# A two-layer RWKV-7 and attention trunk on one core: group norm over eight heads at once, one output-weight pass less, transposes held back

## The chip, the cores and the metric

The kernel runs on one core of one Trainium2 chip. Five engines work side by side: TensorE (PE in the profile; its weight loads are PEld), VectorE (DVE), ScalarE (ACT), GpSimd (POOL) and SyncE (SP), which issues most of the DMAs. The metric is the device time of one execution in microseconds (us); of the kernel before, three runs are known, with a median of 740.5 us.

## The reference

The input is 256 tokens of 1024 numbers. Layer 0 is an RWKV-7 time mix and a SwiGLU feed-forward, layer 1 is attention and a second feed-forward; behind each of the four stands a layer norm over `ALPHA * x + sublayer(x)`. The part that matters here is the end of the time mix and the start of the first feed-forward:

```python
_, y = lax.scan(step, S0, ...)                       # recurrence over 256 tokens, 16 heads of 64
mean = y.mean(-1, keepdims=True)                     # group norm: per token and head
var = jnp.square(y - mean).mean(-1, keepdims=True)
y = ((y - mean) * lax.rsqrt(var + GN_EPS)).reshape(B, T, C) * gn_g + gn_b
bonus = jnp.sum(rh * kh * r_k, -1, keepdims=True) * vh
y = (y + bonus.reshape(B, T, C)).astype(x.dtype)
h = (y * g) @ w_o
...
x = layer_norm(ALPHA * x + h, ln_mix_g[i], ln_mix_b[i])
gate, up = jnp.split(x @ w_in, 2, axis=-1)
x = layer_norm(ALPHA * x + (silu(gate) * up) @ w_down, ln_ffn_g[i], ln_ffn_b[i])
```

## The kernel before

**Split weights.** Every product is made in three parts to keep float32 accuracy: a weight block of 512 KB lands in a buffer `raw` (three of them in a ring), ACT casts it to a high part `hi`, and DVE or POOL makes the low part `lo = raw - hi`. The activations have the same two parts (`xhi`, `xlo`; or `xw` with both). TensorE then adds hi by xhi, lo by xhi and hi by xlo. `Stream` does this for a list of blocks in a fixed order (`weight_specs`). A block of kind "split" uses one of four rotating pairs of hi and lo buffers, so the fifth such block waits until the first has been used for the last time; a block of kind "keep" has buffers of its own. `PL` says which blocks POOL makes the low part of, `LATER` which low parts wait for a named event, and `W.hold` which blocks are not cast before a named event.

**Time mix.** The recurrence goes over four chunks of 64 tokens and two groups `f` of eight heads; TensorE makes z, u, s and y of each step, ACT and DVE copy them out (`UV`, `S`, `zs`, `y`). Tokens are handled in two halves `hf` of 128. `group_norm(hf, f)` normalises y of one half and one group of eight heads: with `bn_stats` and `bn_aggr` head by head, a root on ACT, a subtraction and a product on DVE; then TensorE transposes the result (`yt`), DVE multiplies by the gate `gT` and adds `Q` (`yg`), and the two parts are written to `xs0` (`xhi`, `xlo`).

**Output product and norm.** `dense0` multiplies `xs0` by the output weights `w_o` (`wo0`): for each half eight blocks (two column halves `cb` by four row quarters `q`), 48 matmuls of 512 columns into two banks `o`. In the kernel before, the four blocks of `cb` 1 are kept for both halves, and the four of `cb` 0 are loaded and split twice. `norm_and_turn` then does the layer norm on DVE in `xtok` (a token half at a time), and each normalised 512 columns are transposed by TensorE (`tr`) and split into `xw`.

**First feed-forward.** The first four blocks of `in0` are the weights of the first two hidden tiles; they are multiplied token half by token half (`gn`, 48 matmuls of 256 columns for each half), and from there on come matmuls of both halves at once (`gu`, `acc`). `hidden_half` makes the activation of the first two tiles and transposes it (`ht`).

**Order of the work.** A planner (`Issue.run`) sets the order in which instructions are issued. Work is written as generators that yield what they wait for; at each step the planner takes, of those that are ready by its own clock (`Clock`), the one of the lowest rank (the first number of `I.add`). `fence` makes the later instructions of an engine stand behind the earlier ones in the built program. Each engine runs its instructions in this fixed order, so one that waits holds all behind it.

Of the kernel before, what the change touches and what calls it, by code (L numbers as in the profile page):

```python
# [65 lines left out]
BON = 'pool'  # L66
BONW = 'T'
ORDERED = False
PL = {'wo1': [], 'in1': [], 'qkv': [7, 11], 'wo0': [1, 2, 4, 6], 'k': [2], 'r': [0], 'v': [2, 3, 4, 5, 6, 7], 'g2': [0, 1], 'w2': [], 'in0': [5]}
LATER = {'wo0': {11: 'n00'}, 'in0': {0: 'x10'}, 'qkv': {3: 'n10', 4: 'x21', 5: 'x21', 6: 'x21'}, 'in1': {0: 'n20', 1: 'x30', 2: 'x30', 3: 'x30'}}  # L70
LD = {}
MIXV = 'pool'
MIXG = 'pool'
# [326 lines left out]
def weight_specs(a):  # L400
    assert FIRST <= LAG <= min(TAIL)
    specs = []

    def s1(name, key, idx, kind="split", cols=128):
        specs.append((name, kind, KT, cols, 128, a[key][idx]))

    def s2(name, key, cb, kind="split"):
        for q in range(4):
            specs.append((name, kind, 2, 512, 128, a[key][cb * 4 + q]))

    def ffn(i):
        for n in range(2 * FIRST):
            specs.append((f"in{i}", "split", 4, 256, 128, a[f"w_if{i}"][n]))
        for j in range(FIRST, NJ):
            for u in range(2):
                s1(f"in{i}", f"w_in{i}", (j - FIRST) * 2 + u)
            if LAG <= j < NJ - TAIL[i] + LAG:
                specs.append((f"down{i}", "split", 1, 1024, 128, a[f"w_dn{i}"][j - LAG]))
        for j in range(NJ - TAIL[i], NJ):
            specs.append((f"down{i}", "keep", 1, 1024, 128, a[f"w_dn{i}"][j]))  # L420

    for p in range(KT):
        s1("k", "w_k", p, "native" if p < 2 else "split")
        if p == W2AT:
            for n in range(2):
                specs.append(("w2", "keep", 1, 1024, 128, a["w_2"][n]))
        if p == SELAT:
            specs.append(("sel", "cast", KT, 128, 48, a["selT"]))
    for p in range(KT):
        s1("r", "w_r", p)  # L430
    s2("v", "w_v", 0)
    s1("g1", "w_g1a", 0, "native")
    s1("g1", "w_g1b", 0, "native", 96)
    specs.append(("g2", "split", 1, 1024, 128, a["w_g2a"]))
    specs.append(("g2", "stack", 1, 1024, 96, a["w_g2b"]))
    s2("v", "w_v", 1)
    s2("wo0", "w_o0", 0)
    s2("wo0", "w_o0", 1, "keep")
    s2("wo0", "w_o0", 0)
    ffn(0)  # L440
    for n, cb in enumerate((0, 2, 4, 1, 3, 5)):
        s2("qkv", "w_qkv", cb, "keep" if n == 0 else "split")
    for q in range(4):
        for cb in range(2):
            specs.append(("wo1", "keep" if HELD <= q and not (RING and q >= 2) else "split", 2, 512, 128, a["w_o1"][cb * 4 + q]))
    ffn(1)
    return specs
# [3 lines left out]
def trunk(ctx, tc, a, out):  # L451
# [16 lines left out]
    def nm(s):  # L468
        uid[0] += 1
        return f"{s}{uid[0]}"  # L470
# [16 lines left out]
    def ev(name):  # L487
        return E.setdefault(name, Event())
# [4 lines left out]
    for i in range(2):  # L493
        at = [n for n, x in enumerate(W.specs) if x[0] == f"in{i}"][0]
        nxt = [n for n in range(at + 2 * FIRST, len(W.specs)) if W.specs[n][1] == "split"]
        for n in range(2 * FIRST):
            W.hold[nxt[n]] = ev(f"held{i}{n}")

# [148 lines left out]
                I.reach(end, x)  # L647
            yield 0.0

    def norm_and_turn(ev_in, hps, x, gb, xs, half, done, cuts, end=None):  # L650
        yield ev_in
        if len(xs) == 4:
            parts = [(x[:, :, 0, TOK[half]], x[:, :, 1, TOK[half]]) for x in xs]
        else:
            parts = [(x[0][:, :, TOK[half]], x[1][:, :, TOK[half]]) for x in xs]
        m = len(parts) // 2
        fin = count(2 * m, lambda: I.reach(done, *(x[1] for x in parts)))

        def turned(q):
            def part():  # L660
                yield x[:, q * 512:(q + 1) * 512]
                v = turn(x, q, "tr")
                for n in range(m):
                    I.add(1, split(*parts[q * m + n], v[:, n * 4 // m:(n + 1) * 4 // m, :], done=fin))
            I.add(1, part())
        yield from layer_norm(hps, x, gb, cuts, turned, end)
# [538 lines left out]
    xs0 = pieces()  # L1205

    def group_norm(hf, f):
        st = sm.tile([128, 8, 6], F32, tag="gst", name=nm("gst"))
        mv = sm.tile([128, 8, 2], F32, tag="gmv", name=nm("gmv"))
        rs = sm.tile([128, 8], F32, tag="grs", name=nm("grs"))  # L1210
        y = yt[hf][:, f * 8:f * 8 + 8, :]
        yield ev(f"y{hf}{f}")
        for h0 in range(0, 8, 4):
            yield I.idle("DVE")
            for h in range(h0, h0 + 4):
                dve.bn_stats(st[:, h, :], y[:, h, :])
            for h in range(h0, h0 + 4):
                dve.bn_aggr(mv[:, h, :], st[:, h, :])
        yield mv
        act.activation(rs, mv[:, :, 1], AF.Sqrt, bias=eps_gn, scale=1.0)  # L1220
        dve.tensor_tensor(y, y, mv[:, :, 0:1].to_broadcast([128, 8, HD]), ALU.subtract)
        yield rs
        dve.reciprocal(rs, rs)
        dve.tensor_tensor(y, y, rs[:, :, None].to_broadcast([128, 8, HD]), ALU.mult)
        yield y
        yield ev(f"Q{hf}{f}")
        v = turn(yt[hf].rearrange("p h d -> p (h d)"), f, "yt")
        yield v
        m = sm.tile([128, 4, 128], F32, tag="w2", name=nm("yg"), bufs=6)
        dve.tensor_tensor(m, v, gT[f][:, :, TOK[hf]], ALU.mult)  # L1230
        dve.tensor_tensor(m, m, Q[f][:, :, TOK[hf]], ALU.add)
        xh, xl = (x[:, :, TOK[hf]] for x in xs0[f])
        yield from split(xh, xl, m)
        I.reach(ev(f"xy{hf}{f}"), xl)
# [56 lines left out]
    def dense0():  # L1291
# [99 lines left out]
        for hf in range(2):  # L1391
            res[hf] = [bank("o") for _ in range(2)]
            todo = [(0, q) for q in range(4)] + [(1, q) for q in range(4)]
            if hf == 1:
                todo = [(cb, q) for q0 in (0, 2) for cb in (1, 0) for q in (q0, q0 + 1)]
            for cb, q in todo:
                yield ev(f"xy{hf}{q // 2}")
                if (hf, cb) == (1, 1):
                    w = kept[q]
                else:  # L1400
                    w = yield from W.get("wo0")
                    if cb == 1:
                        kept.append(w)
                mm_s2(res[hf][cb], w, xs0, q * 2, hf, q == 0, q == 3)
                yield 0.0
            if xn is None:
                yield ev("rec")
                l0.close()
                pools["fp"] = ctx.enter_context(tc.tile_pool(name="fp", bufs=2))
                xn = wide_pieces()  # L1410
            I.add(1, norm_and_turn(ev(f"h0{hf}"), res[hf][::1 - 2 * hf], xtok[hf], gb, xn, hf, ev(f"x1{hf}"), WIDE[::1 - 2 * hf], ev(f"n0{hf}")))
            I.reach(ev(f"h0{hf}"), *res[hf])
        return xn, xtok

# [1 line left out]
    def ffn(i, xs, evs, finish):  # L1416
# [62 lines left out]
        for hf in range(2):  # L1479
            ps = bank("gn")[:, :FIRST * 256]  # L1480
            for n in range(2 * FIRST):
                if hf == 0:
                    ws.append((yield from W.get(f"in{i}")))
                if n == 0:
                    yield evs[hf]
                j, q = n // 2, n % 2
                m = 0
                for k in range(4):
                    x = xs[q * 2 + k // 2][:, k % 2]
                    for ww, xx in ((ws[n][0], x[:, 0]), (ws[n][1], x[:, 0]), (ws[n][0], x[:, 1])):  # L1490
                        mm(ps[:, j * 256:(j + 1) * 256], xx[:, TOK[hf]], ww[:, k, :],
                           start=(q + m == 0), stop=(q == 1 and m == 11))
                        m += 1
                if hf == 1:
                    I.reach(ev(f"held{i}{n}"))
                yield 0.0
            I.add(1, hidden_half(hf, ps))
        for j in range(FIRST, NJ):
# [102 lines left out]
    def dense1(xs, xtok):  # L1601
# [59 lines left out]
                    yield 0.0  # L1661
        xn = wide_pieces()
        for hf in range(2):
            I.add(1, norm_and_turn(ev(f"h1{hf}"), res[hf], xtok[hf], gb, xn, hf, ev(f"x3{hf}"), WIDE, ev(f"n2{hf}")))
            if hf == 1:
                for cb in range(2):
                    for q in range(HELD, 4):
                        out_part(hf, q, cb)
                        yield 0.0
            I.reach(ev(f"h1{hf}"), *res[hf])  # L1670
# [52 lines left out]
    I.add(6, bonus())  # L1723
    for hf in range(2):
        for f in range(2):
            I.add(7, group_norm(hf, f))
    I.add(30, dense())
    I.run()

# [82 lines left out]
```

## Time and profile before

| | us |
|---|---|
| runs | 739.4, 740.5, 740.72 |
| profiled execution, its own time | 739.19 |
| its span, first to last instruction | 737.4 |
| PE busy | 681.3 (92%) |
| DVE busy | 531.4 (72%) |
| ACT busy | 392.9 (53%) |
| POOL busy | 139.3 (19%) |

The times in the profile run from the span's first instruction, so the span is what moves when the chain of waits gets shorter, and 1.8 us lie around it. A share of busy time is a mean over stages with different limits; the chain that ended last is 67% PE and 19% DVE. The mean clock granted to TensorE is 0.969 of full speed.

### The profile page before, as it was taken

The numbers are of one execution on the slowest core, as the hardware profiler recorded it, in microseconds if no ns is written. First come the engines' busy times: TensorE is split into PE (matmuls) and PEld (weight loads), VectorE is DVE, ScalarE is ACT, GpSimd is POOL, SyncE is SP. The second block draws the span as 40 slices with busy tenths as digits, with TensorE's granted clock in tenths as the row PEclk, the third lists the DMA queues.
The fourth block names the chain that finished last, engine by engine and source line by source line (L and its number), as shares of the span: only waits on it lengthen the run. The fifth ranks groups of instructions, "written<-read, shape, count | busy, mean of one in ns | idle before, by whom it ended". The sixth has DMA issues, their size and how long they took to land.

```text
span 737.4 us, 11797 instructions
## 1 busy us (share of the span) xinstructions
PE 681.3 (92%) x4500; PEld 582.2 (79%) x4500; DVE 531.4 (72%) x933; ACT 392.9 (53%) x712; POOL 139.3 (19%) x111
## 2 busy tenths in 40 slices
PE   6899695898787999999999899999989999999995
PEld 5899684777667888888888677777778888888885
DVE  7989999839995756656567945968587666656566
ACT  5984454565353554554556435766646555454550
POOL 5677964451400100000000023110000000000000
PEclk9999898899997999999999999999999999999998
DMA  6445313030564655555556545346046565555541
GB/s 245 154 146 191 105 33 115 30 116 33 174 207 152 228 187 184 197 182 192 196 178 229 172 147 178 133 140 200 2 172 213 189 198 179 191 183 189 199 145 57
DMA packets 33576, 117.21 MB, mean 159 GB/s; under 512 B 3808, under 2 KB 4832, under 8 KB 33520
## 3 DMA queue, kind: packets, MB, share of 16 engines
q1 hardware_dynamic: 31936, 110.89, 45.4%
q10 hardware_dynamic: 1584, 5.57, 2.2%
q8 instruction: 35, 0.57, 0.3%
q14 instruction: 21, 0.17, 0.1%
HBM read 115.40 MB, written 1.05 MB: 158 GB/s over the span
## 4 chain that ended last, share of the span: by engine, by line
PE 67%; DVE 19%; DMA 5%; ACT 3%; issue 3%; POOL 2%; DVEq 0%; SPq 0%; ACTq 0%; POOLq 0%
PE gu L328 29%; PE acc L328 14%; PE qkv L328 8%; DVE lo L328 4%; PE gn L328 3%; PE o L328 3%; DVE TT L328 2%; DVE tmp L328 2%; ACT hi L328 2%; PE k L328 2%; DVE xtok L328 1%; DMA raw<-in_w_qkv_dram 1%; DMA raw<-in_w_dn_dram 1%; DVE mx L328 1%; PE pv L328 1%
## 5 line engine op out<-in xcount | busy, mean ns | idle before, releaser
L328 DVE TENSOR_TENSOR lo<-raw,hi 128x1024 fp32r<-128x1024 f32 (+1 forms) x193 | 231.8, 1208 | 151.4 <-ACT hi L328 151.0
L328 ACT CAST hi<-raw 128x1024 fp32r<-128x1024 f32 (+1 forms) x213 | 211.9, 1002 | 174.2 <-issue 78.5
L328 PE MATMUL gu<-xw,hi 128*128 128x512 f32 x640 | 226.0, 394 | 0.0
L328 PE MATMUL gu<-xw,lo 128*128 128x256 f32 x640 | 180.4, 282 | 0.0
L328 PEld LDWEIGHTS gu<-xw,hi 128*128 128x128 f32 x640 | 120.2, 188 | 26.6
L328 PEld LDWEIGHTS gu<-xw,lo 128*128 128x128 f32 x640 | 120.5, 188 | 0.8
L328 POOL TENSOR_TENSOR lo<-raw,hi 128x1024 fp32r<-128x1024 f32 (+1 forms) x20 | 41.6, 2088 | 240.0 <-ACT hi L328 239.5
L328 PE MATMUL acc<-hi,hh 128*128 128x512 f32 (+1 forms) x180 | 53.7, 368 | 0.3 <-ACT hh L328 0.3
L328 PE MATMUL acc<-lo,hh 128*128 128x512 f32 (+1 forms) x180 | 53.7, 368 | 0.0
L328 PE MATMUL acc<-hi,hl 128*128 128x512 f32 (+1 forms) x180 | 53.7, 368 | 0.0
L328 PE MATMUL qkv<-hi,xhi 128*128 128x512 f32 x96 | 39.9, 416 | 2.7 <-ACT xhi L328 2.7
L328 ACT ACTIVATE silu<-silu 128x256 f32<-128x256 f32 x40 | 16.7, 418 | 44.0 <-DVE silu L328 44.0
L328 PE MATMUL qkv<-lo,xhi 128*128 128x512 f32 x96 | 38.6, 402 | 0.0
L328 PE MATMUL qkv<-hi,xlo 128*128 128x512 f32 x96 | 38.6, 402 | 0.0
L328 PEld LDWEIGHTS acc<-hi,hl 128*128 128x128 f32 x180 | 32.8, 188 | 6.3 <-DVE hl L328 0.2
L328 PEld LDWEIGHTS acc<-lo,hh 128*128 128x128 f32 x180 | 32.7, 188 | 5.9
L328 PEld LDWEIGHTS acc<-hi,hh 128*128 128x128 f32 x180 | 31.7, 188 | 6.5 <-ACT hh L328 0.7
L328 PE MATMUL o<-hi,xhi 128*128 128x512 f32 x64 | 26.1, 416 | 2.8 <-ACT xhi L328 2.8
L328 PE MATMUL gn<-hi,xw 128*128 128x256 f32 x128 | 27.0, 307 | 0.1
L328 PE MATMUL o<-hi,xlo 128*128 128x512 f32 x64 | 25.8, 403 | 1.2 <-DVE xlo L328 1.2
L328 PE MATMUL o<-lo,xhi 128*128 128x512 f32 x64 | 26.5, 413 | 0.0
L328 PEld LDWEIGHTS qkv<-hi,xhi 128*128 128x128 f32 x96 | 18.5, 193 | 6.9 <-ACT xhi L328 2.9
(229 smaller groups left out, 1258.1 us busy)
## 6 DMA issues: line engine op xcount, KB each, us to landing
raw<-in_w_in_dram SPq DMA_DIRECT2D x80, 512.0 KB, 3.4
raw<-in_w_dn_dram SPq DMA_DIRECT2D x44, 512.0 KB, 3.4
raw<-in_w_qkv_dram SPq DMA_DIRECT2D x24, 512.0 KB, 3.5
raw<-in_w_o_dram SPq DMA_DIRECT2D x20, 512.0 KB, 3.4
raw<-in_w_r_dram SPq DMA_DIRECT2D x8, 512.0 KB, 3.3
raw<-in_w_v_dram SPq DMA_DIRECT2D x8, 512.0 KB, 3.3
raw<-in_w_if_dram SPq DMA_DIRECT2D x8, 512.0 KB, 3.4
raw<-in_w_k_dram SPq DMA_DIRECT2D x6, 512.0 KB, 3.4
```

The lines of the kernel that those rows point to most:

```text
L328: ins = f(*args, **kw).ins
```

## The change

Three things are changed, and they are all between the recurrence and the second token half of the first feed-forward tiles (one line does the same for layer 1).

1. `group_norm` sums over eight heads at once: one `tensor_reduce` over 128x512 gives the sums, one `scalar_tensor_tensor` subtracts the means, ACT squares the result, a second `tensor_reduce` sums the squares. For the first token half its rank goes from 7 to 4, ahead of the recurrence with 5.
2. The `wo0` blocks are eight and not twelve: all are used for both token halves. Of these POOL splits two, and not four. The first four `in0` blocks are held until the second half's products of `cb` 0 have been issued.
3. The transposes of the second token half wait (`gate`) until the `gn` products of the first half have been issued, with fences on PE; those of the first half wait for a place in the last output products.

```diff
-PL = {..., 'wo0': [1, 2, 4, 6], ...}
-LATER = {'wo0': {11: 'n00'}, 'in0': {0: 'x10'}, ...}
+PL = {..., 'wo0': [1, 2], ...}
+LATER = {'in0': {0: 'x10', 1: 'x10'}, ...}
...
     s2("wo0", "w_o0", 0)
     s2("wo0", "w_o0", 1, "keep")
-    s2("wo0", "w_o0", 0)
...
+        for n in range(4 if i == 0 else 0):
+            W.hold[at + n] = ev(f"held2{n}")
...
-    def norm_and_turn(ev_in, hps, x, gb, xs, half, done, cuts, end=None):
+    def norm_and_turn(ev_in, hps, x, gb, xs, half, done, cuts, end=None, gate=None):
...
+                if gate is not None:
+                    yield gate
                 yield x[:, q * 512:(q + 1) * 512]
...
-        for h0 in range(0, 8, 4):
-            yield I.idle("DVE")
-            for h in range(h0, h0 + 4):
-                dve.bn_stats(st[:, h, :], y[:, h, :])
-            for h in range(h0, h0 + 4):
-                dve.bn_aggr(mv[:, h, :], st[:, h, :])
-        yield mv
-        act.activation(rs, mv[:, :, 1], AF.Sqrt, bias=eps_gn, scale=1.0)
-        dve.tensor_tensor(y, y, mv[:, :, 0:1].to_broadcast([128, 8, HD]), ALU.subtract)
+        yield I.idle("DVE")
+        dve.tensor_reduce(st, y, AX.X, ALU.add)
+        dve.scalar_tensor_tensor(y, st[:, :, None].to_broadcast([128, 8, HD]), -1.0 / HD, y, ALU.mult, ALU.add)
+        yield y
+        sq = sm.tile([128, 8, HD], F32, tag="w2", name=nm("gsq"), bufs=6)
+        act.activation(sq, y, AF.Square)
+        yield sq
+        dve.tensor_reduce(rs, sq, AX.X, ALU.add)
+        yield rs
+        act.activation(rs, rs, AF.Sqrt, bias=eps_gn, scale=1.0 / HD)
...
-                todo = [(cb, q) for q0 in (0, 2) for cb in (1, 0) for q in (q0, q0 + 1)]
+                todo = [(cb, q) for q0 in (0, 2) for cb in (0, 1) for q in (q0, q0 + 1)]
...
-                if (hf, cb) == (1, 1):
-                    w = kept[q]
+                if hf == 1:
+                    w = kept[cb * 4 + q]
                 else:
                     w = yield from W.get("wo0")
-                    if cb == 1:
-                        kept.append(w)
+                    kept.append(w)
                 mm_s2(res[hf][cb], w, xs0, q * 2, hf, q == 0, q == 3)
+                if (hf, cb) == (1, 0):
+                    I.reach(ev(f"held2{q}"))
+                if (hf, cb, q) == (1, 1, 2):
+                    pe.fence()
+                    I.reach(ev("o00"))
+                if hf == 1 and (cb, q) == todo[-1]:
+                    pe.fence()
...
-            I.add(1, norm_and_turn(..., res[hf][::1 - 2 * hf], ..., WIDE[::1 - 2 * hf], ev(f"n0{hf}")))
+            I.add(1, norm_and_turn(..., res[hf], ..., WIDE, ev(f"n0{hf}"), ev("gn0") if hf else ev("o00")))
...
                 if hf == 1:
                     I.reach(ev(f"held{i}{n}"))
+                elif n == 2 * FIRST - 1:
+                    pe.fence()
+                    I.reach(ev(f"gn{i}"))
...
-            I.add(1, norm_and_turn(ev(f"h1{hf}"), ..., WIDE, ev(f"n2{hf}")))
+            I.add(1, norm_and_turn(ev(f"h1{hf}"), ..., WIDE, ev(f"n2{hf}"), ev("gn1") if hf else None))
...
-            I.add(7, group_norm(hf, f))
+            I.add(7 if hf else 4, group_norm(hf, f))
```

In the built program the rows of every engine are the same in both kernels up to the recurrence's third chunk, and again from the second half's `gn` products on. In between, three places move. The first is DVE at the end of the recurrence. `UV_140<-u` is the copy by which the recurrence's last chunk goes on; the second of the two (u_2100 before, u_2103 now) is DVE's last instruction of the recurrence; y_141 and y_142 are the token halves, and xlo_148 is the first operand of the output product that DVE writes. Before:

```order
L328 SCALAR_TENSOR_TENSOR Q_145<-bo_2069,vec,gT_143 128x128 x2
L328 COPY UV_140<-u_2100 64x256
L328 SCALAR_TENSOR_TENSOR Q_145<-bo_2069,vec,gT_143 128x128 x2
L328 TENSOR_TENSOR y_141<-y_141,grs_175 128x512
L328 BN_STATS gst_176<-y_142 128x6 x4
L328 BN_AGGR gmv_177<-gst_176 128x2 x4
L328 BN_STATS gst_176<-y_142 128x6 x2
L328 SCALAR_TENSOR_TENSOR Q_146<-bo_2152,vec,gT_144 128x128 x4
L328 TENSOR_TENSOR yg_2198<-yt_2188,gT_143 128x512
L328 TENSOR_TENSOR yg_2201<-yt_2193,gT_144 128x512
L328 TENSOR_TENSOR yg_2198<-yg_2198,Q_145 128x512
L328 TENSOR_TENSOR yg_2201<-yg_2201,Q_146 128x512
```

Now:

```order
L328 TENSOR_TENSOR yg_2059<-yt_2039,gT_143 128x512
L328 TENSOR_TENSOR y_141<-y_141,grs_172 128x512
L328 TENSOR_TENSOR yg_2059<-yg_2059,Q_145 128x512
L328 COPY UV_140<-u_2050 64x256
L328 TENSOR_TENSOR yg_2112<-yt_2097,gT_144 128x512
L328 TENSOR_TENSOR xlo_148<-yg_2059,xhi_147 128x4x128
L328 TENSOR_TENSOR yg_2112<-yg_2112,Q_146 128x512
L328 COPY UV_140<-u_2103 64x256
L328 SCALAR_TENSOR_TENSOR Q_145<-bo_1949,vec,gT_143 128x128 x4
L328 TENSOR_REDUCE gst_174<-y_142 128x8
```

The first half's `yg` and xlo_148 have moved from behind the recurrence's last copy to ahead of it, and the 128x6 and 128x2 instructions are gone.

The second place is TensorE at the layer norm (xtok_2216 before and xtok_2140 now are the second token half; gn_2502 and gn_2422 are the first half's feed-forward products, gn_2495 the second half's). Before:

```order
L328 MATMUL o_2379<-hi_2412,xlo_150 128x512
L328 MATMUL o_2379<-hi_2412,xhi_149 128x512
L328 MATMUL o_2379<-lo_2413,xhi_149 128x512
L328 MATMUL o_2379<-hi_2412,xlo_150 128x512
L328 MATMUL tr_2528<-cst,xtok_2216 128x128 x4
L328 MATMUL tr_2536<-cst,xtok_2216 128x128 x4
L328 MATMUL gn_2502<-hi_2423,xw_2375 128x256
L328 MATMUL gn_2502<-lo_2424,xw_2375 128x256
L328 MATMUL gn_2502<-hi_2423,xw_2375 128x256 x2
L328 MATMUL gn_2502<-lo_2424,xw_2375 128x256
```

Now:

```order
L328 MATMUL gn_2422<-lo_2424,xw_2304 128x256
L328 MATMUL gn_2422<-hi_2423,xw_2304 128x256 x2
L328 MATMUL gn_2422<-lo_2424,xw_2304 128x256
L328 MATMUL gn_2422<-hi_2423,xw_2304 128x256
L328 MATMUL tr_2498<-cst,xtok_2140 128x128 x4
L328 MATMUL tr_2508<-cst,xtok_2140 128x128 x4
L328 MATMUL ht_2513<-cst,sg_2496 128x128 x2
L328 MATMUL gn_2495<-hi_2277,xw_2301 128x256
L328 MATMUL gn_2495<-lo_2278,xw_2301 128x256
L328 MATMUL gn_2495<-hi_2277,xw_2301 128x256 x2
```

The second half's two sets of transposes stood ahead of all `gn` products and now stand between the first half's and the second half's.

The third place is DVE between the first half's layer norm (xtok_2215, xtok_2139) and the split of its transposed result (xw). Before:

```order
L328 BN_STATS lnst_2393<-xtok_2215 128x6
L328 TENSOR_TENSOR lo_2391<-raw_2342,hi_2390 128x2x256
L328 BN_AGGR lnmv_2398<-lnst_2393 128x2
L328 SCALAR_TENSOR_TENSOR xtok_2215<-xtok_2215,lnmv_2398,gb_2219 128x512
L328 RECIPROCAL lnrs_2400<-lnrs_2400 128x1
L328 SCALAR_TENSOR_TENSOR xtok_2215<-xtok_2215,lnmv_2398,gb_2219 128x512
L328 SCALAR_TENSOR_TENSOR xtok_2215<-xtok_2215,lnrs_2400,gb_2221 128x512 x2
L328 TENSOR_TENSOR lo_2413<-raw_2356,hi_2412 128x2x256 x2
L328 TENSOR_TENSOR xw_2375<-tr_2452,xw_2375 128x2x128
```

Now:

```order
L328 RECIPROCAL lnrs_2314<-lnrs_2314 128x1
L328 SCALAR_TENSOR_TENSOR xtok_2139<-xtok_2139,lnmv_2312,gb_2143 128x512
L328 SCALAR_TENSOR_TENSOR xtok_2139<-xtok_2139,lnrs_2314,gb_2145 128x512 x2
L328 TENSOR_TENSOR xlo_150<-yg_2321,xhi_149 128x4x128
L328 TENSOR_TENSOR lo_2353<-raw_2275,hi_2352 128x1024
L328 TENSOR_TENSOR lo_2278<-raw_2232,hi_2277 128x1024
L328 TENSOR_TENSOR lo_2340<-raw_2256,hi_2339 128x1024
L328 TENSOR_TENSOR xw_2301<-tr_2388,xw_2301 128x2x128
L328 SCALAR_TENSOR_TENSOR xtok_2140<-xtok_2140,o_2305 128x512
L328 TENSOR_TENSOR xw_2302<-tr_2388,xw_2302 128x2x128
```

Where one low part (of the last `w_o` block) stood, three low parts of `in0` blocks stand now, the third block's first; `xw` and the second half's layer norm (xtok_2140) are queued behind them.

## Rows read from the trace of the kernel before

**Rows 1.** Chain that ended last, in order of time: start, us, what.

```profile
226.53 1.97 PE tr L328 x8
228.50 11.13 PE gn L328 x84
...
241.27 4.20 PE gu L328 x24
```

**Rows 2.** Busy us of PE, PEld, DVE, ACT, POOL by stretch; PEclk, DMA share, GB/s.

```profile
184.00:227.10 43.10, 30.52 (x175) 23.62 (x173) 41.17 (x98) 19.20 (x36) 8.88 (x6) 0.89 0.62 201
226.50:231.00 4.50, 4.47 (x21) 4.47 (x22) 3.28 (x6) 2.60 (x5) 0.00 (x0) 0.50 0.81 245
231.00:241.30 10.30, 10.30 (x88) 10.30 (x87) 2.16 (x3) 3.88 (x6) 1.88 (x1) 1.00 0.15 54
241.30:390.00 148.70, 148.70 (x793) 128.00 (x793) 93.17 (x129) 78.18 (x129) 0.52 (x1) 1.00 0.58 193
```

**Rows 3.** Who waited for whom, 187 to 228.5 us: total, times, longest.

```profile
PE tr L328 <- DVE xtok L328: 8.5, 1, 8.5
```

**Rows 4.** Timeline of DVE: start, us, instruction, count, idle before it.

```profile
183.58 0.43 DVE L328 COPY UV<-u 64x256 f32<-64x256 f32 x1
...
186.34 1.13 DVE L328 SCALAR_TENSOR_TENSOR Q<-bo,vec,gT 128x128 f32<-128x128 f32 x4
...
192.36 0.58 DVE L328 BATCH_NORM_STATS2 gst<-y 128x6 f32<-128x64 f32 x4
192.85 0.37 DVE L328 BATCH_NORM_AGGREGATE gmv<-gst 128x2 f32<-128x6 f32 x4
193.25 1.21 DVE L328 TENSOR_TENSOR y<-y,gmv 128x512 f32<-128x512 f32 x1
...
204.36 0.68 DVE L328 TENSOR_TENSOR yg<-yt,gT 128x512 f32<-128x512 f32 x1
204.96 0.68 DVE L328 TENSOR_TENSOR lo<-raw,hi 128x512 fp32r<-128x512 f32 x1
...
222.59 1.22 DVE L328 TENSOR_TENSOR lo<-raw,hi 128x1024 fp32r<-128x1024 f32 x1
223.73 0.75 DVE L328 SCALAR_TENSOR_TENSOR xtok<-xtok,lnmv,gb 128x512 f32<-128x512 f32 x1
224.39 1.22 DVE L328 TENSOR_TENSOR lo<-raw,hi 128x1024 fp32r<-128x1024 f32 x1
...
225.72 1.41 DVE L328 SCALAR_TENSOR_TENSOR xtok<-xtok,lnrs,gb 128x512 f32<-128x512 f32 x2
```

**Rows 5.** Timeline of POOL, 184 to 245 us.

```profile
192.63 6.42 POOL L328 TENSOR_TENSOR lo<-raw,hi 128x512 fp32r<-128x512 f32 x4 [4.04 <-ACT hi L328]
```

**Rows 6.** Groups of DVE by form: busy us, mean ns; idle before.

```profile
L328 DVE TENSOR_REDUCE nmx<-sc 128x1 f32<-128x256 f32 x16 | 6.5, 408 | 0.0
...
L328 DVE TENSOR_REDUCE nmx<-sc 128x1 f32<-128x128 f32 x16 | 4.4, 274 | 0.0
```

**Rows 7.** Timeline of DVE in layer 1, at the same place.

```profile
546.01 1.40 DVE L328 SCALAR_TENSOR_TENSOR xtok<-xtok,lnrs,gb 128x512 f32<-128x512 f32 x2
```

**Rows 8.** Timeline of PE in layer 1, at the same place.

```profile
547.51 1.04 PE L328 MATMUL tr<-cst,xtok 128*128 128x128 f32 x8
...
555.25 0.40 PE L328 MATMUL gu<-xw,hi 128*128 128x512 f32 x1
```

**Rows 9.** Timeline of PE, output products of layer 0.

```profile
197.01 0.39 PE L328 MATMUL o<-hi,xlo 128*128 128x512 f32 x1
197.24 0.39 PE L328 MATMUL o<-hi,xhi 128*128 128x512 f32 x1
```

**Rows 10.** Timeline of ACT and its DMA queue (ACTq), same stretch.

```profile
189.91 0.82 ACTq L328 DMA_DIRECT2D xtok<-in_x_dram  x2
...
214.14 1.06 ACT L328 CAST hi<-raw 128x1024 fp32r<-128x1024 f32 x1 [0.96 <-DMA raw<-in_w_if_dram]
```

**Rows 11.** DMA issues, 155 to 250 us: count, KB each, us to landing.

```profile
raw<-in_w_if_dram SPq DMA_DIRECT2D x4, 512.0 KB, 3.9
```

More of the change, by code (lines that the diff above doesn't have):

```diff
@@ L68 @@
 ORDERED = False
-PL = {'wo1': [], 'in1': [], 'qkv': [7, 11], 'wo0': [1, 2, 4, 6], 'k': [2], 'r': [0], 'v': [2, 3, 4, 5, 6, 7], 'g2': [0, 1], 'w2': [], 'in0': [5]}
-LATER = {'wo0': {11: 'n00'}, 'in0': {0: 'x10'}, 'qkv': {3: 'n10', 4: 'x21', 5: 'x21', 6: 'x21'}, 'in1': {0: 'n20', 1: 'x30', 2: 'x30', 3: 'x30'}}
+PL = {'wo1': [], 'in1': [], 'qkv': [7, 11], 'wo0': [1, 2], 'k': [2], 'r': [0], 'v': [2, 3, 4, 5, 6, 7], 'g2': [0, 1], 'w2': [], 'in0': [5]}
+LATER = {'in0': {0: 'x10', 1: 'x10'}, 'qkv': {3: 'n10', 4: 'x21', 5: 'x21', 6: 'x21'}, 'in1': {0: 'n20', 1: 'x30', 2: 'x30', 3: 'x30'}}
 LD = {}
@@ L1207, in group_norm @@
     def group_norm(hf, f):
-        st = sm.tile([128, 8, 6], F32, tag="gst", name=nm("gst"))
-        mv = sm.tile([128, 8, 2], F32, tag="gmv", name=nm("gmv"))
+        st = sm.tile([128, 8], F32, tag="gst", name=nm("gst"))
         rs = sm.tile([128, 8], F32, tag="grs", name=nm("grs"))
@@ L1410, in dense0 @@
                 xn = wide_pieces()
-            I.add(1, norm_and_turn(ev(f"h0{hf}"), res[hf][::1 - 2 * hf], xtok[hf], gb, xn, hf, ev(f"x1{hf}"), WIDE[::1 - 2 * hf], ev(f"n0{hf}")))
+            I.add(1, norm_and_turn(ev(f"h0{hf}"), res[hf], xtok[hf], gb, xn, hf, ev(f"x1{hf}"), WIDE, ev(f"n0{hf}"), ev("gn0") if hf else ev("o00")))
             I.reach(ev(f"h0{hf}"), *res[hf])
@@ L1663, in dense1 @@
         for hf in range(2):
-            I.add(1, norm_and_turn(ev(f"h1{hf}"), res[hf], xtok[hf], gb, xn, hf, ev(f"x3{hf}"), WIDE, ev(f"n2{hf}")))
+            I.add(1, norm_and_turn(ev(f"h1{hf}"), res[hf], xtok[hf], gb, xn, hf, ev(f"x3{hf}"), WIDE, ev(f"n2{hf}"),
+                                    ev("gn1") if hf else None))
             if hf == 1:
```

## The prediction

> **What bounds the kernel now.** Read the chain of waits in order of time first, around the place that the change touches. From 241.27 us on it is TensorE on the first feed-forward; before that stand the `gn` products from 228.50 and eight transposes from 226.53 [rows 1]. The table by stretches says what each side of that point is limited by: from 241.3 to 390 PE is busy for all of 148.70 us, so whatever brings the first `gu` matmul forward moves everything behind it by as much. From 184 to 227.1 DVE is busy for 41.17 of 43.1 us and PE for 30.52, so this stretch is DVE's [rows 2]. The table of waits has the price on PE: the transposes of the second token half waited 8.5 us for DVE's `xtok`, and all `gn` products, also those of the first half, whose input was ready, were queued behind them [rows 3]. The clock has a part in it: behind that idle stretch PEclk is 0.50, the 1.2 GHz level, until 231, and 1.00 afterwards [rows 2].
>
> So the time of the first `gu` matmul is the sum of two stretches. A: from DVE's last instruction of the recurrence, which ends at 183.58 + 0.43 = 184.0, to the end of the second half's layer norm at 225.72 + 1.41 = 227.1 [rows 4]: 43.1 us. B: from there to 241.27 [rows 1]: 14.1 us.
>
> **Stretch A, part by part.** I count DVE's work in the new order, from its last copy of the recurrence to the end of the second half's layer norm, by start-to-start steps of the timeline.
> - 128x512 instructions over two inputs step at 204.96 - 204.36 = 0.60 [rows 4]. There are 31: four group-norm sums, two subtractions of means, two products with the root, four `yg`, three `xlo`, eight halves of `w_o` low parts, four additions `xtok`+`o`, four statistics of the layer norms. 18.6 us.
> - The layer norms' eight scaled instructions at 224.39 - 223.73 = 0.66: 5.3 us [rows 4].
> - Eight `Q`, at 1.13 for four: 2.3 us [rows 4].
> - Four whole low parts of `in0` at 223.73 - 222.59 = 1.14: 4.6 us [rows 4].
> - Four splits `xw` of half the 512 columns, taken at 0.35, and six tiny ones (roots inverted, layer-norm aggregates) taken at 0.12: estimates from the rows above, 2.1 us.
>
> That is 32.9 us of work. The sums are not in this trace at 128x512. The two reductions that are take 274 ns for 128 columns and 408 for 256 [rows 6], 134 for each further 128, which gives 408 + 268 = 676 ns at 512, as the 0.68 that the two-input ones last. The bounds: 0.41 from the row of 256 below, 1.21 above, the longest that a 128x512 instruction of this group norm took [rows 4]. I take 0.68, since both rows lie on one line. The Trainium skill speaks against the change here: its page VectorE: DVE Perf Modes, section Rules for kernel authors, calls `tensor_reduce` on a hot path the slowest operation of this engine. If that meant the upper end it would be a result of its own, which is the fourth rival.
>
> To the work come waits. One is new: the third `in0` block can be cast only when the third `w_o` block of `cb` 0 has been used for the second half, and its low part now stands in DVE's order ahead of the two others, of `xw` and of the second half's layer norm. From the second half's first `xlo`, PE needs 26 products to that point, at 197.24 - 197.01 = 0.23 each [rows 9], 6.0 us, then ACT 1.06 for the cast [rows 10]; DVE has 4.8 us of work in that time (the rest of the first half's layer norm, the second `yg` and `xlo`). It waits 2.3 us, and all behind it with it. Lower bound: none, if PE gets there early; upper bound: 8.3, if these products run at the lower clock level, where a product takes twice as long (PEclk 0.50 against 1.00 [rows 2]).
>
> The blocks themselves are not late: their buffers come free as the `w_o` low parts are written, and landing takes 3.9 us [rows 11], which ends some 7 us before that cast. Leaving four loads out gains nothing on the path by itself.
>
> The start of stretch A also moves. The first half's group norm now goes ahead of the recurrence. Two groups cost DVE eight instructions of 0.60 and two inversions, 5.0 us, and its `yg` and first `xlo`, five of 0.60, come before the last copy: 8.0. They replace two sets of statistics (0.49 for four and 0.40 for four aggregates [rows 4], hence 1.8 a group), two subtractions, one product and two `Q`: about 6.0. Up to 2 us later, then, or not at all where DVE had room; I take 1.5. On ACT the squares add four instructions of this size, and ACT is busy for 19.20 of 43.1 us [rows 2], so they are hidden; if that cover is gone, each costs its length, near 0.6. The token rows and gains are now fetched by ACT ahead of the recurrence's last copies out; two issues took 0.82 [rows 10], so four hold ACT's queue for 1.6 us, behind which the second half's second group norm starts. DVE has the `Q` and the first sum to do meanwhile.
>
> Sum: 184.0 + 1.5 + 32.9 + 2.3 = 220.7, against 227.1: 6.4 us less. Two low parts move from POOL to DVE, which my list holds; for them POOL's four halves (6.42 us [rows 5]) go, beside which one `y` product of DVE took 1.21 [rows 4]. The Trainium skill (GPSIMD Engine Reference, section Specifications) says that GpSimd shares its interface to SBUF with VectorE; the trace agrees with 1.21 against 0.68, and the sum doesn't use it.
>
> **Stretch B.** Of the 14.1 us the first half's 48 `gn` products now run while DVE is at the second half's layer norm. What is left (transposes, splits, 48 products) is what layer 1 does already, where `tr` stands between the halves: from 546.01 + 1.40 = 547.4 to the first `gu` at 555.25 [rows 7, 8], 7.8 us. So 6.3 us less. From single rows it would be 48 products at 10.30 / 88 = 0.117 [rows 2], 5.6, and about 0.8 for the transposes and splits, 6.4 in all; I take the measured 7.8. In layer 1 the built order stays as it is, so the new gate there is worth nothing.
>
> **Sum.** 6.4 + 6.3 = 12.7 us. The profiled execution took 739.19, span 737.4 with 1.8 around it; less 12.7 that is 726.5. The median of the runs, 740.5, is 1.3 above it, so the forecast is 727.8.
>
> **The rivals.**
> 1. No waits in A: the recurrence no later and the cast in time, 1.5 + 2.3 less: 724.0. For it: DVE's order has other work at both points. Against it: PE's 26 products can't start before the second half's `xlo`.
> 2. The second half's output products run at the lower clock. PE waits twice for DVE just before them, and behind a long wait it has fallen to 0.50 [rows 2, 3]. The new wait becomes 8.3 instead of 2.3: 733.8. Against it: these waits are 1 to 2 us by my count, and not 8.5.
> 3. The held transposes buy nothing, since the `in0` low parts behind the new wait are late and the first half's products start only with the second half's. Then A's 6.4 alone are left: 734.1. Against it: the order puts these low parts before the second half's layer norm.
> 4. A reduction takes 1.21: eight of them, four in the recurrence and four in A, 0.53 more each than 0.68: 4.2 us, 732.0. Against it: [rows 6].
> 5. Slower: PE stays at 1.2 GHz from the first output product on, since these now come in short runs among DVE's pieces. The place is PE from about 185 to `gu`; the price 88 products (the rest of 96 ran so already) at 0.23 more, 20 us, and some 75 `gn` at 0.117, 9 us. Once this work, 22 us of `o`, 11 of `gn` and 3 of transposes at full speed, doubles, PE ends near 185 + 72 = 257, 16 us later than now: 756. It decides when PE's work here passes 241.3 - 185 = 56 us, that is, when more than half of it runs at the low level. Against it: the recurrence, with shorter matmuls and waits among them, is not what the clock fell behind; the idle 8.5 us were.
>
> **How the numbers follow.** Forecast 0.60, with a range of its own of 725 to 731; rivals 1 to 4: 0.12, 0.11, 0.05, 0.06; rival 5: 0.06, of which 0.02 lie near its point of decision. The range from 723.5 to 734 takes in rivals 1, 2 and 4 and leaves out some 0.15. Faster by over 0.2% (about what a measurement of this kernel tells from no change): 0.94; within 0.2%: 0.02; slower: 0.04.
>
> **What would show it.** In the profile after: the first `gu` matmul near 228.5; the first half's `gn` before the second half's transposes, starting near 214, and PE's wait for `xtok` down to about 2 us; the second half's layer norm ending near 221; output products starting near 185; a 128x512 reduction near 0.68; DVE idle about 2 us ahead of the third `in0` block's low part, released by ACT's cast. Wrong would be the sum if `gu` starts beyond 234, and its reasons, if DVE is not busy almost throughout from 185 to 221, or if layer 1 differs by more than a few tenths.

## The result, and the profile after

The changed kernel takes 728.03 us in the median of its runs (726.73 to 728.42 and one of 733.24), the kernel before 740.61 beside it: a ratio of 0.9846, 95% interval 0.9823 to 0.9869. The profiled execution took 727.64 us with a span of 725.9; the forecast was 727.8. Run again later beside three experiments it took 728.24, ratio 0.9840 (0.9824 to 0.9855).

The end of the chain of waits after, around the first `gu` product (start, us, what), answers to [rows 1]:

```profile
222.06 0.67 PE tr L328 x4
...
223.91 5.59 PE gn L328 x46
229.50 4.21 PE gu L328 x24
```

`gu` starts at 229.50 for 241.27. Only 46 `gn` products stand between the transposes and it, where 84 stood. The table by stretches (length, then busy us of PE, PEld, DVE, ACT and POOL, then PEclk, DMA share, GB/s) answers to [rows 2]:

```profile
184.00:227.10 43.10, 39.91 (x283) 32.45 (x280) 38.25 (x72) 20.56 (x41) 2.46 (x2) 1.00 0.53 179
185.50:203.90 18.40, 15.98 (x98) 11.65 (x96) 18.30 (x38) 9.08 (x19) 2.46 (x2) 1.00 0.71 247
203.90:215.30 11.40, 11.38 (x54) 9.38 (x55) 8.46 (x14) 4.30 (x7) 0.00 (x0) 1.00 0.14 47
215.30:229.30 14.00, 13.24 (x106) 12.25 (x106) 10.66 (x22) 8.50 (x15) 1.29 (x1) 1.00 0.63 198
228.50:390.00 161.50, 161.50 (x863) 138.78 (x862) 101.43 (x139) 85.92 (x141) 1.92 (x1) 1.00 0.60 196
```

In the stretch that was VectorE's, TensorE is now the busier engine: 39.91 of 43.1 us for 30.52. From the first output product to `gu` it is idle for 2.4 + 0.0 + 0.8 us, and its clock stays at 1.00, where before it stood at 0.50 behind the idle 8.5 us. From 228.5 on it never pauses, as before.

Who waited for whom, 184 to 229 us (total, times, longest), answers to [rows 3]:

```profile
DVE lo L328 <- ACT hi L328: 4.3, 2, 2.9
PE o L328 <- DVE xlo L328: 1.3, 1, 1.3
PE tr L328 <- DVE xtok L328: 0.5, 1, 0.5
```

The transposes' wait of 8.5 us has become 0.5. The new wait on VectorE is there, 2.9 us. The timeline of VectorE (start, us, instruction, count, idle before it) answers to [rows 4]:

```profile
185.94 0.43 DVE L328 COPY UV<-u 64x256 f32<-64x256 f32 x1
186.40 1.13 DVE L328 SCALAR_TENSOR_TENSOR Q<-bo,vec,gT 128x128 f32<-128x128 f32 x4
187.44 0.68 DVE L328 TENSOR_REDUCE gst<-y 128x8 f32<-128x512 f32 x1
...
207.76 0.68 DVE L328 TENSOR_TENSOR xlo<-yg,xhi 128x512 fp32r<-128x512 f32 x1
211.38 3.50 DVE L328 TENSOR_TENSOR lo<-raw,hi 128x1024 fp32r<-128x1024 f32 x3 [2.94 <-ACT hi L328]
...
221.26 1.41 DVE L328 SCALAR_TENSOR_TENSOR xtok<-xtok,lnrs,gb 128x512 f32<-128x512 f32 x2
```

Stretch A now runs from 186.37 to 222.67, 36.3 us for 43.1; stretch B from there to 229.50, 6.8 us for 14.1. A reduction of 128x512 takes 0.68. In layer 1 the order is the same; its stretch from the layer norm to `gu` takes 8.1 us for 7.8.

### The profile page after: what moved, and what is told of

Its sections match the earlier page's. It is cut to its first block, busy times and chain, and to the rows that moved or that the text cites. A ratio compares the mean times of both kernels' runs of the same rounds, so it can differ in the third digit from the quotient of the medians.

```text
span 725.9 us, 11712 instructions
## 1 busy us (share of the span) xinstructions
PE 679.7 (94%) x4500; PEld 579.0 (80%) x4500; DVE 524.1 (72%) x873; ACT 390.4 (54%) x709; POOL 131.3 (18%) x107
## 4 chain that ended last, share of the span: by engine, by line
PE 69%; DVE 19%; ACT 4%; issue 3%; DMA 2%; POOL 1%; SPq 0%; DVEq 0%; ACTq 0%; POOLq 0%
PE gu L328 30%; PE acc L328 15%; PE qkv L328 8%; DVE lo L328 4%; PE o L328 3%; DVE xtok L328 2%; DVE TT L328 2%; PE gn L328 2%; DVE tmp L328 2%; PE k L328 2%; ACT hi L328 1%; PE pv L328 1%; PE v L328 1%; POOL lo L328 1%; PE att L328 1%
## 5 line engine op out<-in xcount | busy, mean ns | idle before, releaser
L328 DVE TENSOR_TENSOR lo<-raw,hi 128x1024 fp32r<-128x1024 f32 (+1 forms) x189 | 228.9, 1218 | 154.7 <-ACT hi L328 154.5
L328 ACT CAST hi<-raw 128x1024 fp32r<-128x1024 f32 (+1 forms) x206 | 207.7, 1014 | 173.6 <-issue 84.3
L328 POOL TENSOR_TENSOR lo<-raw,hi 128x1024 fp32r<-128x1024 f32 (+1 forms) x16 | 34.5, 2164 | 231.8 <-ACT hi L328 231.4
```

What stands on the lines that cost most here:

```text
L328: ins = f(*args, **kw).ins
```

## The experiments

Two theories went in. HOLD is what the prediction said of stretch B: the hold on the second half's transposes lets the first half's `gn` products run beside the layer norm. EARLY BLOCKS says that TensorE's order is not enough: the `gn` products can run early only because the low parts of in0's blocks now stand ahead of that layer norm in VectorE's queue. From x10 on a third was tested, TENSORE-BOUND: once nothing breaks TensorE's run of work, `gu` follows from its first output product. (The expectations of x1 and x5 speak of 40 `gn` products for each half; there are 48.)

Executions differ by up to 2.5 us before the place of the change, so the traces are compared from one instruction on, the end of the `UV` copy that VectorE starts at 160 to 162.5 us (160.40 in the kernel before). From it to the first `o` product, the end of the second half's layer norm and the first `gu`, by the timelines. Each run stands beside the kernel before on the same chip; where that differs, the ratios compare and not the medians.

| kernel | median us (before beside it) | ratio, 95% interval | first o | norm ends | gu |
|---|---|---|---|---|---|
| before | | | 29.57 | 66.73 | 80.71 |
| changed (x8) | 728.24 (740.32) | 0.9840, 0.9824 to 0.9855 | 24.83 | 62.02 | 68.73 |
| x1 hold alone | 742.43 (740.34) | 1.0037, 1.0015 to 1.0058 | 29.58 | 66.60 | 82.73 |
| x2 weights alone | 729.85 (740.34) | 0.9870, 0.9848 to 0.9893 | 29.58 | 62.91 | 69.75 |
| x3 norm alone | 733.08 (740.34) | 0.9907, 0.9887 to 0.9927 | 24.84 | 68.34 | 76.24 |
| x4 changed, no hold | 730.63 (740.34) | 0.9870, 0.9843 to 0.9898 | 24.85 | 62.19 | 69.21 |
| x5 block 0 late | 735.90 (740.32) | 0.9938, 0.9924 to 0.9953 | 24.85 | 60.27 | 76.07 |
| x6 new norm, no head start | 734.36 (740.32) | 0.9923, 0.9907 to 0.9939 | 34.49 | 66.14 | 73.37 |
| x7 low parts in turn | 728.44 (740.32) | 0.9836, 0.9817 to 0.9855 | 24.84 | 60.36 | 68.44 |
| x9 old norm, head start | 733.09 (739.28) | 0.9906, 0.9889 to 0.9923 | 25.99 | 65.03 | 71.81 |
| x10 old norm, no head start | 729.24 (739.28) | 0.9858, 0.9840 to 0.9875 | 29.56 | 63.07 | 69.87 |
| x11 half a head start | 730.09 (739.28) | 0.9872, 0.9855 to 0.9888 | 27.19 | 62.03 | 69.96 |
| x12 one block to GpSimd | 727.98 (740.89) | 0.9822, 0.9797 to 0.9847 | 24.85 | 60.62 | 67.96 |

**x1, the hold alone.** The kernel before, with gates on layer 0's transposes (and the events that they wait for, with the fences on PE) and nothing else:

```diff
+                if gate is not None:
+                    yield gate
                 yield x[:, q * 512:(q + 1) * 512]
...
-            ... WIDE[::1 - 2 * hf], ev(f"n0{hf}")))
+            ... WIDE[::1 - 2 * hf], ev(f"n0{hf}"), ev("gn0") if hf else ev("o00")))
```

> The kernel before, with nothing but the hold: the second half's transposes of layer 0 may stand only behind the first half's 40 gate/normalisation products (gn). Theory EARLY BLOCKS: the gain behind the second half's layer norm does not come from the hold but from the split weight blocks of in0 standing ahead of that layer norm in VectorE's queue. Here they don't: the low part of block 0, which the first gn product needs, is still queued behind the layer norm, so gn starts at about 228.3 us as before (228.15), the 8 transposes now follow it at about 234.5, the other 40 gn products after them, and gu starts at about 242 (before 241.3). Time 741 to 742 us, no change within 0.2%. Rival HOLD, which is what the prediction said: the hold itself lets gn run beside the layer norm; gu at 234 to 235, time 733 to 734.5 us.

742.43 us: 2.1 slower, just above the 741 to 742 of EARLY BLOCKS and far from HOLD's 733 to 734.5. TensorE's timeline in x1 shows why:

```profile
219.53 0.28 PE L328 MATMUL gn<-hi,xw 128*128 128x256 f32 x1
230.03 0.58 PE L328 MATMUL gn<-lo,xw 128*128 128x256 f32 x1 [10.23 <-DVE lo L328]
...
237.24 1.03 PE L328 MATMUL tr<-cst,xtok 128*128 128x128 f32 x8
```

And VectorE's there:

```profile
227.43 1.42 DVE L328 SCALAR_TENSOR_TENSOR xtok<-xtok,lnrs,gb 128x512 f32<-128x512 f32 x2
228.76 1.22 DVE L328 TENSOR_TENSOR lo<-raw,hi 128x1024 fp32r<-128x1024 f32 x1
```

The order did as the hold wants: `gn` first, transposes behind. But the second product needs the low part of block 0, and that is made at 228.76, behind the layer norm. TensorE waits 10.2 us for it instead of 8.5 for `xtok`. HOLD fails.

**x2, the weights alone.** The change without its group norm and without any hold on transposes, in either layer; against the changed kernel:

```diff
-            I.add(1, norm_and_turn(..., WIDE, ev(f"n0{hf}"), ev("gn0") if hf else ev("o00")))
+            I.add(1, norm_and_turn(..., WIDE, ev(f"n0{hf}"), None))
...
-            I.add(7 if hf else 4, group_norm(hf, f))
+            I.add(7, group_norm(hf, f))
```

with `group_norm` as in the kernel before. The fences on PE and the holds on in0's casts stay.

> The change without its group norm and without any hold: output weights of layer 0 split once (8 blocks for 12), old group norm behind the recurrence. EARLY BLOCKS: VectorE splits two blocks less (2 x 1.25 us), three of in0's blocks stand ahead of the second half's layer norm, so the first half's gn products run beside it although nothing holds the transposes: layer norm ends 224.6 to 227, gu 231.5 to 234.5, time 731 to 734 us. HOLD: without the hold only the 2.5 us of splitting go: 738 us.

729.85, 10.5 us faster: nearly the whole gain, and more than the 731 to 734 us expected. TensorE's timeline in x2:

```profile
222.87 0.38 PE L328 MATMUL gn<-lo,xw 128*128 128x256 f32 x1 [0.22 <-DVE lo L328]
...
225.21 1.27 PE L328 MATMUL tr<-cst,xtok 128*128 128x128 f32 x8 [0.78 <-PE gn L328]
...
232.62 0.39 PE L328 MATMUL gu<-xw,hi 128*128 128x512 f32 x1
```

And VectorE's:

```profile
216.62 1.22 DVE L328 TENSOR_TENSOR lo<-raw,hi 128x1024 fp32r<-128x1024 f32 x1
...
218.09 1.22 DVE L328 TENSOR_TENSOR lo<-raw,hi 128x1024 fp32r<-128x1024 f32 x1
...
221.61 1.21 DVE L328 TENSOR_TENSOR lo<-raw,hi 128x1024 fp32r<-128x1024 f32 x1
...
224.37 1.41 DVE L328 SCALAR_TENSOR_TENSOR xtok<-xtok,lnrs,gb 128x512 f32<-128x512 f32 x2
```

Without any gate the transposes stand behind the first half's `gn`, since these are ready: all four of in0's low parts (one more starts at 214.81) are made before the layer norm ends.

**x3, the norm alone.** The kernel before with the new `group_norm` and `I.add(7 if hf else 4, ...)`.

> The kernel before with nothing but the new group norm, begun inside the recurrence for the first half (12 blocks, no hold). EARLY BLOCKS: the recurrence ends about 2 us later, VectorE saves 4 x 0.5 us and has the first half's norm behind it, and all four in0 blocks now stand ahead of the second half's layer norm: that norm ends 2 to 5 us earlier (222 to 225), gu 229 to 232, time 728.5 to 732 us. HOLD: only VectorE's part, 736 to 738.5 us.

733.08, 7.3 us faster, just short of the expected 728.5 to 732; `gu` comes 4.5 us earlier in its trace, whose execution (735.75) was the slowest of six. The 2.8 us by which the two gains differ stay open. TensorE's timeline in x3, then VectorE's:

```profile
229.50 0.41 PE L328 MATMUL gn<-hi,xw 128*128 128x256 f32 x1
229.71 1.91 PE L328 MATMUL tr<-cst,xtok 128*128 128x128 f32 x8
```

```profile
225.91 1.23 DVE L328 TENSOR_TENSOR lo<-raw,hi 128x1024 fp32r<-128x1024 f32 x1 [4.06 <-ACT hi L328]
...
228.68 1.41 DVE L328 SCALAR_TENSOR_TENSOR xtok<-xtok,lnrs,gb 128x512 f32<-128x512 f32 x2
```

Here too in0's low parts moved ahead of the layer norm, and stretch B is 7.9 us; the norm itself ends 1.6 us later, behind a new wait of 4.06 us on a cast. So what this edit gains lies in stretch B, as EARLY BLOCKS has it, though less came at `gu` than expected. The order of TensorE is that of the hold, `gn` first and transposes behind, and this kernel has neither the gates nor the fences of the change: once the low parts are early, the planner makes this order by itself.

**x4, no hold.** In the changed kernel both gates of layer 0 become `None`, as in x2.

> The changed kernel with the hold taken out of layer 0 (both halves). EARLY BLOCKS: the second half's transposes stay behind the first half's gn products all the same; the first half's go ahead of 22 of the second half's o products, where TensorE may wait up to 2 us for them, and the low part of in0's block 2 moves behind the first of the second half's sums, so that VectorE's wait of 2.9 us goes: 727 to 729.5 us, gu 228.5 to 231. HOLD: the transposes are back in the way, gu at 235 to 236, time 734 to 735 us.

730.63 (727.13 to 733.80). In the trace `gu` is 0.5 us later than in the changed kernel, not 6 to 7. VectorE's wait of 2.9 us is gone, as expected, but waits of 0.95, 1.46 and 0.35 us came in its place. The two intervals overlap, so whether the hold is worth nothing or up to 2 us isn't settled; HOLD's 734 to 735 is out. The transposes stand behind the first half's `gn` here as well (223.89 us).

**x5, block 0 late.** The changed kernel, its hold kept, with one table entry that moves one VectorE instruction behind the layer norm:

```diff
-LATER = {'in0': {0: 'x10', 1: 'x10'}, ...
+LATER = {'in0': {0: 'n01'}, ...
```

> The changed kernel with one VectorE instruction elsewhere: the low part of in0's block 0 may be made only behind the second half's layer norm (TensorE's order stays, the hold too). EARLY BLOCKS: the layer norm ends about 2 us earlier (220.5 for 222.7, since that instruction no longer stands ahead of it and block 1's fits into the wait), but the first gn product waits for it until about 221.7, the 40 products then take 5.6, the transposes and casts about 2, the other 40 products 5.6: gu at 234.5 to 235.5 (229.3 now), 732.5 to 734 us against the changed kernel's 728. HOLD: gn is still ahead of the transposes, so nothing is lost: 726 to 728 us.

735.90, 7.7 us slower than the changed kernel beside it. TensorE's timeline and two of its stretches (columns as above) in x5:

```profile
222.05 0.58 PE L328 MATMUL gn<-lo,xw 128*128 128x256 f32 x1 [6.70 <-DVE lo L328]
...
229.01 1.04 PE L328 MATMUL tr<-cst,xtok 128*128 128x128 f32 x8
...
236.66 0.39 PE L328 MATMUL gu<-xw,hi 128*128 128x512 f32 x1
```

```profile
222.00:225.00 3.00, 2.95 (x14) 2.95 (x15) 0.00 (x0) 0.00 (x0) 0.00 (x0) 0.50 0.64 197
225.00:229.00 4.00, 4.00 (x35) 4.00 (x35) 0.00 (x0) 0.00 (x0) 0.00 (x0) 1.00 0.00 0
```

This settles stretch B. It is 15.8 us again although the layer norm ends 1.75 us earlier than in x8. `gu` is 1.2 us beyond what was expected. The first half's products take 7.0 us for 5.6, and that is the clock: behind 6.7 idle us it is at the 1.2 GHz level for 3 us, 0.21 a product, and then at full speed with 0.114.

**x6, no head start.** The changed kernel with `I.add(7, group_norm(hf, f))`.

> The changed kernel with the first half's group norm back behind the recurrence (new group norm, weights split once, hold kept). If the head start is what shortens VectorE's stretch: the recurrence ends 2.1 us earlier, but five to eight us of VectorE work come back behind it, o products start at about 190 for 185.5: gu 3 to 5 us later than the changed kernel, 731 to 733 us. If VectorE's stretch is set by its amount of work alone (EARLY BLOCKS with the weights part as the whole gain): what the recurrence loses to the head start is what the stretch gains, 726.5 to 728.5 us.

734.36, 6 us slower and above the 731 to 733 expected. TensorE's timeline in x6:

```profile
192.90 1.08 PE L328 MATMUL yt<-cst,y 128*128 128x128 f32 x4 [5.16 <-DVE grs L328]
194.16 1.09 PE L328 MATMUL yt<-cst,y 128*128 128x128 f32 x4 [0.18 <-DVE y L328]
194.90 0.78 PE L328 MATMUL o<-hi,xhi 128*128 128x512 f32 x1
```

All four groups are done beside each other, and the first output product stands behind the transposes of the last. It comes 9.7 us later than in the changed kernel; from there to `gu` TensorE needs 38.9 us for 43.9.

**x7, low parts in turn.** `'in0': {0: 'x10', 1: 'x10', 2: 'x10'}` in the changed kernel.

> The changed kernel with in0's block 2 held like blocks 0 and 1 (one entry of the table), so that VectorE makes the low parts in the order 0, 1, 2, 3 and the two that are ready fill most of the 2.9 us in which it waited for block 2's cast. If that wait is on the path: the layer norm ends 1.5 to 2.4 us earlier, gu at 227.3 to 228.2, time 726 to 727 us. Rival: o's second half ends at 215.3 anyway, and block 3's low part, now also ahead of the layer norm, waits for its cast: no change, 727.5 to 728.5 us.

728.44, no change. VectorE's timeline, then TensorE's, in x7:

```profile
211.34 1.23 DVE L328 TENSOR_TENSOR lo<-raw,hi 128x1024 fp32r<-128x1024 f32 x1 [0.66 <-ACT hi L328]
...
219.54 1.42 DVE L328 SCALAR_TENSOR_TENSOR xtok<-xtok,lnrs,gb 128x512 f32<-128x512 f32 x2
```

```profile
221.30 0.28 PE L328 MATMUL gn<-hi,xw 128*128 128x256 f32 x1
221.42 1.04 PE L328 MATMUL tr<-cst,xtok 128*128 128x128 f32 x8
```

The wait shrinks from 2.94 to 0.66 and the layer norm ends 1.7 us earlier, yet `gu` only 0.3: the transposes now stand behind TensorE's own `gn`. The rival holds, with another reason than its own.

**x8, the changed kernel again.**

> The changed kernel once more, as the measure for the three others on the same chip: 727 to 729 us.

728.24, as expected; it stands in the table as the measure.

**x9 and x10, the old norm in both places.** Both have the weights and the hold; `group_norm` is that of the kernel before, with `I.add(7 if hf else 4, ...)` in x9 and `I.add(7, ...)` in x10.

> The changed kernel with the old group norm's instructions (bn_stats, bn_aggr, subtraction) in the new place: first half begun inside the recurrence, weights split once, hold kept. VectorE has 4 x 0.5 us more. If the place matters and not the instructions: TensorE's first o product still at 185.5 to 186.5, gu within 1.5 us of the changed kernel's 229.3, time 728 to 730 us. Rival, if the instructions carry the norm's part of the gain: 731 to 734 us.

> Weights split once and the hold, with the old group norm behind the recurrence: against x6 (new norm at the same place, 734.4) the instructions alone, against x9 the head start alone, against x2 (no hold, 729.85) the hold alone. TENSORE-BOUND theory (gu is the first o product plus 39 to 40 us of TensorE work, once nothing breaks that run of work): first o at 190.3 as before, gu at 230 to 231, time 729 to 731 us, so the new instructions without the head start cost 3 to 5 us. Rival, that the new instructions save VectorE's time here too: 736 us or more.

With the changed kernel and x6 they make a square. Old norm: 729.24 behind the recurrence, 733.09 begun inside it. New norm: 734.36 and 728.24. Either edit alone costs 4 to 5 us; both together gain about 1 at most (by ratios 0.9858 to 0.9840, intervals that overlap; at `gu` 69.87 to 68.73). The first expectation for x9 missed and its rival came out: the instructions do matter there. In x9 TensorE starts early but waits 2.41 us for a `w_o` low part and 1.19 for `xlo`. x10 came as expected, and beside x2 no worth of the hold can be told (0.9858 and 0.9870, intervals that overlap).

**x11, half a head start.** `I.add(4 if (hf, f) == (0, 0) else 7, ...)` and x7's table.

> The changed kernel with only the first 8 heads of the first half begun inside the recurrence, and in0's low parts in turn (x7). TENSORE-BOUND theory: the recurrence ends about 1 us earlier than in the changed kernel, the first o product comes at 186.5 to 188 for 185.5, but TensorE waits less behind it (changed kernel: 3.2 us of waits between 185.5 and 229.3): gu at 226.5 to 229, time 725.5 to 728.5 us. Rival, if the first product's time decides: 2 us slower than the changed kernel, 730 us.

730.09: missed, and the rival's figure came out. The first product is 2.4 us later, and TensorE's waits don't shrink by as much (42.8 us to `gu` for 43.9). TENSORE-BOUND gives a lower bound of about 39 us, no forecast of the waits.

**x12, one block to GpSimd.** x7 with `'wo0': [1, 2, 6]` in the table of GpSimd's blocks.

> The changed kernel with in0's low parts in turn (x7) and the low part of one more block of layer 0's output weights (number 6) made on GpSimd, which is idle from 192 to 228 us in the changed kernel. TENSORE-BOUND theory: what is left to gain before gu are TensorE's waits for VectorE between 199 and 204 us (0.36, 0.59 and 1.34 us); VectorE has 1.28 us less to do ahead of them, so up to 1.3 us go: 726.5 to 727.5 us. Rival: GpSimd takes 3.2 us for the block (4 of its halves took 6.42 in the kernel before) and slows VectorE beside it, as before, so that nothing is left of it: 728 to 730 us.

727.98, between the two expectations: no change that can be told. VectorE's timeline in x12, then GpSimd's:

```profile
194.86 2.87 DVE L328 TENSOR_TENSOR lo<-raw,hi 128x512 fp32r<-128x512 f32 x2
...
200.11 1.28 DVE L328 TENSOR_TENSOR lo<-raw,hi 128x512 fp32r<-128x512 f32 x2
```

```profile
193.94 1.55 POOL L328 TENSOR_TENSOR lo<-raw,hi 128x512 fp32r<-128x512 f32 x1 [0.75 <-ACT hi L328]
195.86 1.31 POOL L328 TENSOR_TENSOR lo<-raw,hi 128x512 fp32r<-128x512 f32 x1 [0.37 <-ACT hi L328]
```

Beside GpSimd's two halves VectorE's two take 2.87 us for 1.28. The 1.28 that it was spared go there. No version was found that clearly beats the changed kernel.

## Why the prediction was right, and where its reasons were not

The total came out as said: 12.7 us were forecast at `gu`, 11.8 came (241.27 to 229.50), and the end moved with it. That the median came within 0.3 us is in part luck: A gained 1.9 less than forecast and B 1.0 more, and the traced execution took 727.64 for a forecast 726.5, while the median lies 0.4 above it where I took 1.3.

- **Stretch A, its terms.** The recurrence ends 2.1 us later where I took 1.5 (186.37 for 184.01, less the 0.25 by which this execution was late before it). VectorE's work is 36.30 - 2.94 = 33.4 for 32.9, the wait 2.94 for 2.3. So the norm ends at 222.67 for 220.7, and A gained 4.5 for 6.4: three terms, each a little small. Most of this gain, too, comes with the weights' edit: in x2 alone the norm ends 3.8 us earlier, with the whole change 4.7.
- **The reduction** takes 0.68 at 128x512, the value worked out from [rows 6] and what a sum of two inputs costs, so the fourth rival is out. The Trainium skill (VectorE: DVE Perf Modes, Rules for kernel authors) calls it the slowest operation of the engine; here the trace disagrees, with 0.68 for the reduction and 0.68 for `yg`, a product of two inputs of this size in [rows 4]. (The 1.21 of [rows 4] that the prediction also calls a `y` product is the subtraction of the means; no sum changes by it.)
- **Stretch B, its size.** 6.8 us for 7.8, so it gained 7.3 for 6.3. Layer 1, which I took it from, needs 8.1 after the change (535.65 to 543.75); layer 0's second half does better, near the 6.4 that the single rows gave. There the transposes begin 0.6 us ahead of the norm's end (222.06 for 222.67), in layer 1 before the change 0.1 behind it (547.51 for 547.41), and from them to `gu` it is 7.3 us for 7.7; why the latter was not followed. About 2 us of what B gained are the clock, an estimate: at 0.117 each the 21 instructions that took 4.47 us at 0.50 [rows 2] would have taken 2.5.
- **Stretch B, its owner: wrong.** The step said that the first half's `gn` products now run beside the layer norm, and, with the transposes queued ahead of `gn` as the price before, gave that to their being held. x1 has the hold and loses 2.1 us; x2 has no gate and gains 10.5; x5 has all of the change but one low part in time and loses the stretch again. What pays in B is that in0's low parts stand ahead of the layer norm. TensorE's order goes with it, but it came without the gates in x2, x3 and x4, so that early low parts with the transposes ahead of `gn` were never measured. My third rival named that condition ("the in0 low parts are late"), but as a danger to the hold rather than as the cause, and its "Against it" had the reason that counts.
- **"Leaving four loads out gains nothing on the path by itself": asked too narrowly.** The question was only whether loads and buffers were late. The edit that the loads belong to gives 10.5 us (x2): besides 8 blocks for 12 it has another order of the second half's products, holds on in0's casts, and other entries in `PL` and `LATER`, and with it VectorE's order at in0 moved. Which of these parts does so was not separated, so the sentence itself stays untested; x3 has none of them, and the low parts moved there too.
- **The sum of two stretches.** It holds for the change, not for the next microsecond. With the norm earlier by 1.7 us (x7) `gu` gains 0.3, since TensorE's own run ends there too. The first rival's 724.0 could not come by the wait that it took away.
- **The norm and its head start**, which I priced step by step, are together worth about 1 us of the 12 beside the weights (x10 to x8), not clear of noise. The two bring the first product 4.7 us forward, and TensorE gives 3.6 of it back in waits (from first `o` to `gu` 43.9 us, 40.3 in x10).
- **The second and fifth rival** fell by the granted clock, 1.00 from 185.5 on.

## What to carry to other kernels

An order on one engine gains nothing while the operand that it needs is queued late on another: before crediting a hold, look in the queues of all producers for where the first product's operands are made, and price the edits that move those. When a gain is read as a sum of stretches, try each edit alone: here one gave nearly all, one was harmful by itself, and two that cost 4 to 5 us each cost nothing together.

## What the runs showed that was not expected

Two engines writing low parts at once gained nothing: one block given to GpSimd took 2.86 us there and cost VectorE 1.59 more beside it (2.87 for 1.28), more than the 1.28 it was spared; the rival of x12 had expected this, the theory not. And in x5 TensorE's idle time cost more than itself: 6.7 idle us were followed by 3 us at 0.50, in which 14 products ran for the 26 that 0.114 a product allows.
